# First layer's modulation with stationary conditions, and the attention's maximum and value products rewritten

## The chip, the core and the metric

The kernel runs on one core of one Trainium2 chip. Its time is the device time of one launch in microseconds (us), from the first instruction to the last. Each number of the trace comes from one profiled execution, taken by the hardware profiler. The engines are called PE (TensorE, matrix products), PEld (TensorE's loading of stationary weights), DVE (VectorE), ACT (ScalarE), POOL (GpSimd) and SP (SyncE, which issues the DMA transfers). SBUF is the on-chip memory of 128 partitions, PSUM the memory that TensorE writes.

## What is computed

One inference step of a trunk of two layers, for 1024 latent and 128 context tokens of width 1024. Each layer modulates its normalised input with shift, scale and gate, which are a linear map of the SiLU of a condition vector; there are two conditions, one for latent, one for context tokens. Layer 0 mixes tokens by attention, in which 8 heads of latent attention (96 wide) and 8 query heads of grouped attention (64 wide) stand side by side. Layer 1 mixes by a state-space scan and a gated linear unit. Each ends in a feed-forward block with a convolution. What the change touches is this part of the reference:

```python
def modulation(cond, w_mod, b_mod):
    m = jax.nn.silu(cond.astype(jnp.float32)) @ w_mod.astype(jnp.float32) + b_mod.astype(jnp.float32)
    return [t[:, None, :].astype(cond.dtype) for t in jnp.split(m, 6, axis=-1)]

def modulate(h, shift, scale):
    return h * (1 + scale) + shift
...
def attend(q, k, v):
    ...
    scale = 1.0 / math.sqrt(dq)
    def one_block(qi):
        s = jnp.einsum('bqgrd,bkgd->bgrqk', qi.astype(jnp.float32), kf) * scale
        p = jax.nn.softmax(s, axis=-1)
        return jnp.einsum('bgrqk,bkgd->bqgrd', p, vf)
```

## The kernel before

Tokens lie in nine tiles of 128 (eight latent, one context). Products of full precision are made of three products of rounded halves (`mm3`: high x high, high x low, low x high), so most operands exist as a high and a low tile (names ending in h and l). A product in plain float32 (`mm`) is two passes on TensorE, and the trace counts each pass as a matmul.

The stages run one after the other: the prologue (0 to 44 us), the input projection of layer 0 (44 to 313), attention (first transposes 334, last 940), the feed-forward block (960 to 1960), then layer 1.

**Modulation.** The map has six parts of 1024 columns, q = 0 to 5, and reads 1024 rows in eight blocks k of 128. Conditions and small vectors come into `vrows`, one row per 128 values, and are transposed into the columns of `vcol`. The first two parts (shift and scale of the first norm) are made in the prologue by `mod_part` (L125): the two condition columns of block k (`cond(k)`) are the stationary operand, 128x2, the weights move through, 512 columns at a time, all eight k into the same two rows of PSUM; two VectorE additions put the bias on (L135), eight products with a 2x2 unit matrix turn the result into columns, and one VectorE step writes A or B, by which the first norm's output is scaled and shifted. The next three parts (q = 2, 3, 4) are 24 pieces (`mod_piece`) in the projection's order. A piece fetches 128 columns of all 1024 rows (`ring`, 512 KB in runs of 512 bytes), uses them as eight 128x128 stationary operands, moves the two conditions through, and writes a 128x2 result by one VectorE step.

**Projection.** `Plan` (L2373 on) is a list scheduler: each step has an engine, a cost in us, a key (about when it is due), steps it depends on and buffers it takes. It writes one order for each engine, and the engines run it in that order. The keys are sums with the offsets of the table `TI`. The same planner orders attention, with the table `TM`.

**Attention.** There are 32 groups, one for each head and half of the latent queries; a group has four query tiles j and nine key tiles k (slots). For each j TensorE makes the scores in two parts, sa (768 keys) and sb (384 keys). VectorE takes the maximum of sa (L1041), then that of sb and the larger of both times the negative scale (L1046, L1047: `score_max_b`). ScalarE takes the exponentials into the buffer p (8 of them), sb's first (L1054), sa's then (L1061), both with that maximum as the bias. For each slot k TensorE transposes the four p tiles into one PSUM bank tb (L1070), ScalarE rounds it to pth (L1075), VectorE subtracts for the rest, ptl (L1081), and TensorE multiplies both with the values (`values`): v has 128 columns, the high and low halves of 64. In between stand the turning of the next heads' keys and queries (L931 to L946), the copies and outputs of a group (`pv_copy`, `finish_out`), and the context queries' small attention (`post1`, L1139 to L1142). GpSimd and VectorE also prepare constants of layer 1 (L1733 and others).

```python
            nc.vector.tensor_reduce(mx[:, 1:2], sb[:, :384], axis=AX.X, op=OP.max)
            nc.vector.scalar_tensor_tensor(mx[:, 2:3], mx[:, 0:1], mx[:, 1:2], nscale(hd), op0=OP.max, op1=OP.mult)
            ...
            self.mm(pv[:64], v[:, k, :64], l, False, False)
```

Of the kernel before, what the change touches and what calls it, by code (L numbers as in the profile page):

```python
# [8 lines left out]
F32 = mybir.dt.float32  # L9
# [7 lines left out]
D = 1024  # L17
NS = 8
NT = 9
KT = 8  # L20
# [6 lines left out]
TM = {"sa": -0.51, "sb": 1.2, "ma": -0.08, "mb": 0.77, "eb": 2.0, "ea": 3.1, "ta": 0.17, "td": 0.3, "v": 2.27, "pv": 0.25, "f0": 2.8, "f1": 0.1, "ss": 0.25, "pf": 0.0, "ph": 0.3, "pl": 0.6, "win": 0.2}  # L27
# [7 lines left out]
TI = {"win": 0, "hp": 0.34, "x": -3.37, "a": -1.34, "t": 0.99, "c": 2.74, "o": 3.21, "w": 4.11, "m": 3.93, "dm": 1.55, "st": 8.52, "ld": 8.94, "ml": -0.54}  # L35

class Trunk:
# [45 lines left out]
    def setup(self):  # L83
# [10 lines left out]
        rows = c.tile([72, 128], F32, name="vrows")  # L94
        nc.sync.dma_start(rows[0:8], I["c"].rearrange("o (k p) -> (o k) p", p=128))
        nc.sync.dma_start(rows[8:16], I["c_ctx"].rearrange("(k p) -> k p", p=128))
        nc.sync.dma_start(rows[16:32], I["norm1_g"].rearrange("l (k p) -> (l k) p", p=128))
        nc.sync.dma_start(rows[32:48], I["norm2_g"].rearrange("l (k p) -> (l k) p", p=128))
        nc.sync.dma_start(rows[48:72], I["b_mod"][0, 2 * D:5 * D].rearrange("(k p) -> k p", p=128))
        nc.scalar.activation(rows[0:16], rows[0:16], AF.Silu)  # L100
        self.vcol = c.tile([128, 72], F32, name="vcol")
# [7 lines left out]
        for l in range(2):  # L109
            for n in (1, 2)[l:]:  # L110
                self.A[l, n] = c.tile([128, 8, 2], F32, name=f"A{l}{n}")
                self.B[l, n] = c.tile([128, 8, 2], F32, name=f"B{l}{n}")
        self.vrows = rows

    def vec_cols(self, p):

        self.nc.tensor.transpose(p[:, :72], self.vrows, self.ident[:72, :72])
        self.nc.vector.tensor_copy(self.vcol, p[:, :72])
        b = self.vcol[:, 64:72]
        self.nc.vector.tensor_scalar(b, b, 1.0, None, op0=OP.add)  # L120

    def cond(self, k):
        return self.vcol[:, k:k + 9:8]

    def mod_part(self, w, bs, wk, ps2, psv, l, q):  # L125

        nc = self.nc
        rs = []
        for k in range(KT):
            for a in range(2):  # L130
                self.mm(ps2[a][0:2, :], self.cond(k), w(k)[:, a * 512:(a + 1) * 512], k == 0, k == KT - 1)
            yield
        for a in range(2):
            r = wk.tile([128, 512], F32, name="v_t")[0:2]
            nc.vector.tensor_tensor(r, ps2[a][0:2, :], bs[a], op=OP.add)  # L135
            if q in (2, 5):
                nc.sync.dma_start(self.m_rows[l, :, q, a * 512:(a + 1) * 512], r)
            rs.append(r)
        if q in (2, 5):
            return  # L140
        for j in range(KT):
            self.mm(psv[:, 2 * j:2 * j + 2], rs[j // 4][:, j % 4 * 128:(j % 4 + 1) * 128], self.ident[0:2, 0:2], True, True)
        n = 1 if q < 3 else 2
        src = psv[:, :16].rearrange("p (k c) -> p k c", c=2)
        if q % 3 == 0:
            nc.vector.tensor_copy(self.B[l, n], src)
        else:
            g0 = (16 if n == 1 else 32) + 8 * l
            g = self.vcol[:, g0:g0 + 8].unsqueeze(2).to_broadcast([128, 8, 2])
            nc.vector.scalar_tensor_tensor(self.A[l, n], src, 1.0, g, op0=OP.add, op1=OP.mult)  # L150
# [106 lines left out]
    def attn_in(self):  # L257
# [15 lines left out]
        ps = self.pool(st, "ai_ps", bufs=2, space=PSUM)  # L273

# [59 lines left out]

# [2542 lines left out]
```

## Time and profile before

| what | us |
|---|---|
| three runs: median (lowest, highest) | 3208.28 (3203.06, 3208.59) |
| profiled execution | 3213.05 |
| its span, first to last instruction | 3211.3 |
| PE busy in the span | 3078.6 (96%) |
| DVE busy | 2205.0 (69%) |
| ACT busy | 1509.7 (47%) |
| POOL busy | 1106.6 (34%) |

The shares are means over stages that differ, so the rows further below are taken from single stretches. A row of a timeline gives the start, the duration, the engine, the line of the kernel, the operation with output and inputs, its shape (for a matmul the stationary operand, then the moving one) and a count when several alike run together. Matmuls overlap, so a start is subtracted from the next start to get what one costs. A bracket names the idle time ahead of it and what ended that.

### The profile page before, as it was taken

Reading aid. Unit: us, or ns where it says so; the run is one execution under the profiler, and the core shown is the slowest. Engines: PE = TensorE matmul, PEld = TensorE weight load, DVE = VectorE, ACT = ScalarE, POOL = GpSimd, SP = SyncE. Lnnn points to the kernel's source line nnn. Section 1 sums busy time; section 2 is a strip of 40 time slices with the busy share of each in tenths; the row PEclk is TensorE's granted clock in tenths of the full one; section 3 lists DMA queues with packets and bytes.
Section 4 is the critical chain, followed back from the end, with each engine's and each line's share of the span. In section 5 each row is a group of like instructions: output and inputs, shape, how many; then the busy total and the mean of one; then the engine's idle time right before and its main releaser. Section 6 shows DMA issues by size and latency. Waiting matters only on the chain. (4 is left out here: it accounts for less than half of the span.)

```text
span 3211.3 us, 49583 instructions
## 1 busy us (share of the span) xinstructions
PE 3078.6 (96%) x18116; PEld 2771.4 (86%) x18116; DVE 2205.0 (69%) x3936; ACT 1509.7 (47%) x3027; POOL 1106.6 (34%) x1789
## 2 busy tenths in 40 slices
PE   8999888999999999999999998899999999999999
PEld 4999777788878898888888897779999999999998
DVE  3645888888864777887888967773365556656555
ACT  3421766677752344334444445662344444444443
POOL 2645566765022554164516404853320001001000
PEclk8999999999999999999999998999999999999999
DMA  5654212222121546544556646851133444444443
GB/s 207 191 166 122 46 59 74 67 72 96 48 71 60 165 147 199 158 148 147 178 156 197 197 137 165 210 149 55 53 99 120 130 122 141 121 128 139 124 131 99
DMA packets 535532, 408.75 MB, mean 127 GB/s; under 512 B 97765, under 2 KB 495733, under 8 KB 535289
## 3 DMA queue, kind: packets, MB, share of 16 engines
q1 hardware_dynamic: 535288, 405.58, 42.3%
q8 instruction: 143, 2.34, 0.3%
q14 instruction: 101, 0.82, 0.1%
HBM read 351.01 MB, written 54.51 MB: 126 GB/s over the span
## 5 line engine op out<-in xcount | busy, mean ns | idle before, releaser
L52 PE MATMUL ub<-hh,wu_l 128*128 128x386 f32 (+1 forms) x1056 | 359.2, 340 | 10.5 <-DVE wu_l L62 10.5
L52 PE MATMUL ua<-hh,wu_l 128*128 128x386 f32 (+1 forms) x1056 | 358.1, 339 | 0.4 <-DVE wu_l L62 0.4
L52 PE MATMUL ub<-hh,wu_h 128*128 128x386 f32 (+1 forms) x1056 | 357.6, 339 | 0.5 <-ACT wu_h L61 0.5
L52 PE MATMUL ua<-hl,wu_h 128*128 128x386 f32 (+1 forms) x1056 | 357.9, 339 | 0.0
L52 PE MATMUL ub<-hl,wu_h 128*128 128x386 f32 (+1 forms) x1056 | 357.8, 339 | 0.0
L52 PE MATMUL ua<-hh,wu_h 128*128 128x386 f32 (+1 forms) x1056 | 357.3, 338 | 0.2 <-DVE cv_a L2630 0.2
L62 DVE TENSOR_TENSOR wu_l<-wu_raw,wu_h 128x1024 fp32r<-128x1024 f32 x264 | 329.9, 1250 | 37.9 <-ACT wu_h L61 37.8
L2660 POOL TENSOR_TENSOR o<-o,f_h 128x512 f32<-128x512 f32 x16 | 21.7, 1373 | 864.7 <-DVE f_h L2673 864.7
L52 PE MATMUL y<-wd_h,g_h 128*128 128x512 f32 x792 | 319.2, 403 | 0.0
L52 PE MATMUL y<-wd_h,g_l 128*128 128x512 f32 x792 | 312.6, 395 | 0.0
L52 PE MATMUL y<-wd_l,g_h 128*128 128x512 f32 x792 | 312.1, 394 | 0.0
L61 ACT ACTIVATE wu_h<-wu_raw 128x1024 fp32r<-128x1024 f32 x264 | 276.5, 1047 | 32.4 <-PE sa L52 18.3
L2621 ACT ACTIVATE cv_a<-ua,cw 128x384 f32<-128x384 f32 (+1 forms) x132 | 88.7, 672 | 378.1 <-PE ua L52 378.1
L2621 ACT ACTIVATE cv_b<-ub,cw 128x384 f32<-128x384 f32 (+1 forms) x132 | 88.7, 672 | 337.1 <-PE ub L52 337.1
L1075 ACT ACTIVATE pth<-tb 128x512 fp32r<-128x512 f32 x288 | 171.5, 599 | 121.5 <-PE tb L1070 108.2
L1070 PE MATMUL tb<-ident,p 128*128 128x128 f32 x1152 | 178.6, 278 | 35.7 <-DVE ptl L1081 33.1
L52 PEld LDWEIGHTS ub<-hh,wu_l 128*128 128x128 f32 x1056 | 199.0, 188 | 15.2 <-DVE wu_l L62 15.2
L1081 DVE TENSOR_TENSOR ptl<-tb,pth 128x512 fp32r<-128x512 f32 x288 | 193.9, 683 | 26.0 <-ACT pth L1075 23.7
L2629 DVE SCALAR_TENSOR_TENSOR cv_a<-ua,cw,cv_a 128x384 f32<-128x384 f32 (+1 forms) x132 | 81.4, 617 | 182.4 <-ACT cv_a L2621 182.1
L52 PEld LDWEIGHTS ua<-hl,wu_h 128*128 128x128 f32 x1056 | 199.2, 189 | 5.9
L52 PEld LDWEIGHTS ua<-hh,wu_h 128*128 128x128 f32 x1056 | 199.0, 188 | 6.0 <-issue 0.5
L52 PEld LDWEIGHTS ub<-hh,wu_h 128*128 128x128 f32 x1056 | 199.2, 189 | 0.9 <-ACT wu_h L61 0.8
(561 smaller groups left out, 8280.9 us busy)
## 6 DMA issues: line engine op xcount, KB each, us to landing
wu_raw<-in_ffn_w_up_dram SPq DMA_DIRECT2D x264, 512.0 KB
wd_raw<-in_ffn_w_down_dram SPq DMA_DIRECT2D x132, 512.0 KB
mw<-in_w_mod_dram SPq DMA_DIRECT2D x28, 1024.0 KB
ring<-in_w_mod_dram SPq DMA_DIRECT2D x24, 512.0 KB
tab_s<-t_o SPq DMA_DIRECT2D x16, 584.0 KB
tb<-tab_s SPq DMA_DIRECT2D x64, 146.0 KB
m<-in_w_mod_dram SPq DMA_DIRECT2D x8, 1024.0 KB
ca_s<-o SPq DMA_DIRECT2D x16, 512.0 KB
```

What stands on the lines that cost most here:

```text
L52: return self.nc.tensor.matmul(out, lhsT, rhs, start=start, stop=stop)
L61: self.nc.scalar.activation(hi, src, AF.Copy)
L62: self.nc.vector.tensor_tensor(lo, src, hi.bitcast(F32), op=OP.subtract)
L1070: nc.tensor.transpose(t[:, j * 128:(j + 1) * 128], P[hd, a, j][:, k * 128:(k + 1) * 128], self.ident)
L1075: nc.scalar.activation(h, PT[hd, a, k][0], AF.Copy)
L1081: nc.vector.tensor_tensor(l, t, h.bitcast(F32), op=OP.subtract)
L2621: nc.scalar.activation(t[:, :m], p[:, 1:1 + m], AF.Identity, scale=cw[:, 1, cf:cf + 1], bias=cw[:, 3, cf:cf + 1])
L2629: nc.vector.scalar_tensor_tensor(t[:, :m], p[:, 0:m], cw[:, 0, cf:cf + 1], t[:, :m], op0=OP.mult, op1=OP.add)
L2660: e.tensor_tensor(x, x, s, op=OP.add)
```

## The change

**Prologue.** The conditions are copied into `cpad`, 32 columns for each k of which two are filled. `mod_part` holds `cpad[:, k]` stationary in the column tile of partitions 32(k mod 4), so that four k's write four stretches of PSUM partitions and two rounds cover eight. One half is copied out by VectorE, the other by ScalarE, and eight products with `sum4` (128x2, which has ones at the rows of the four tiles) turn and add at once. The bias is added afterwards, as columns, by `mod_set`. Its rows are now part of `vrows` (88 rows).

**Pieces.** A piece fetches 128 rows of all 1024 columns, in rows of 4 KB. It has four products: `cpad[:, n]` stationary in column tile j, 256 of the columns moving. VectorE adds the 128x256 result into `ACC`, and after the eighth piece of a part TensorE transposes `ACC` in two halves and `mod_set` writes the part.

**Attention.** The scale, with a minus sign, goes into the gains `g_gq` and `g_mq` with which the queries are normalised, so scores come out negated; the maximum becomes a minimum, and the exponential's scale is −1. `score_max_b` is one VectorE step that takes the elementwise minimum of sb with sa's minimum, writes it to p as scrap and accumulates the row's minimum. p is therefore taken in that step. The products of v with ptl use all 128 columns. The rotation of queries and keys works in place. The planner's costs and the offsets in `TM` and `TI` are other numbers.

```diff
-TM = {"sa": -0.51, "sb": 1.2, "ma": -0.08, "mb": 0.77, "eb": 2.0, "ea": 3.1, "ta": 0.17, "td": 0.3, "v": 2.27, "pv": 0.25, "f0": 2.8, "f1": 0.1, "ss": 0.25, "pf": 0.0, "ph": 0.3, "pl": 0.6, "win": 0.2}
+TM = {"sa": -1.14, "sb": -0.03, "ma": -1.2, "mb": 0.36, "eb": 1.57, "ea": 3.1, "ta": 0.34, "td": 0.3, "v": 2.27, "pv": 0.89, "f0": 2.8, "f1": 0.1, "ss": 0.35, "pf": 0.0, "ph": 0.3, "pl": 0.6, "win": 0.2}
...
+        nc.vector.tensor_copy(self.cpad[:, :, :2], self.vcol[:, :16].rearrange("p (c k) -> p k c", c=2))
...
+        nc.vector.tensor_reduce(self.sum4, self.ident.rearrange("p (j n) -> p n j", j=4)[:, :2], axis=AX.X, op=OP.add)
...
+        v.tensor_tensor(dst, src, cols(self.mod_bias(q)), op=OP.add)
+        if q in (1, 4):
+            g0 = 16 if q == 1 else 32
+            v.tensor_tensor(dst, dst, cols(self.vcol[:, g0:g0 + 8]), op=OP.mult)
...
-        for k in range(KT):
+        for k0 in (0, 4):
             for a in range(2):
-                self.mm(ps2[a][0:2, :], self.cond(k), w(k)[:, a * 512:(a + 1) * 512], k == 0, k == KT - 1)
-            yield
+                for k in range(k0, k0 + 4):
+                    o = 32 * (k - k0)
+                    self.mm(ps2[a][o:o + 32, :], self.cpad[:, k], w(k)[:, a * 512:(a + 1) * 512], k0 == 0, k0 > 0)
         for a in range(2):
-            r = wk.tile([128, 512], F32, name="v_t")[0:2]
-            nc.vector.tensor_tensor(r, ps2[a][0:2, :], bs[a], op=OP.add)
...
+            r = wk.tile([128, 512], F32, name="v_t")
+            if a:
+                nc.scalar.activation(r, ps2[a], AF.Copy)
+            else:
+                nc.vector.tensor_copy(r, ps2[a])
+            for j in range(4 * a, 4 * a + 4):
+                self.mm(psv[:, 2 * j:2 * j + 2], r[:, j % 4 * 128:(j % 4 + 1) * 128], self.sum4, True, True)
+        self.mod_set(q, (self.B if q == 0 else self.A)[0, 1], psv[:, :16].rearrange("p (k c) -> p k c", c=2))
...
+        g.tensor_scalar(g_gq, g_gq, -1.0 / math.sqrt(64), None, op0=OP.mult)
+        g.tensor_scalar(g_mq, g_mq, -1.0 / math.sqrt(96), None, op0=OP.mult)
...
-                w = S[name] = raw().rearrange("p (k n) -> p k n", k=KT)
-                nc.sync.dma_start(w, wm[:, :, q * D + n * 128:q * D + (n + 1) * 128])
+                w = S[name] = raw()
+                nc.sync.dma_start(w, wm[n, :, q * D:(q + 1) * D])
...
-                for k in range(KT):
-                    self.mm(p[:, :2], w[:, k], self.cond(k), k == 0, k == KT - 1)
+                for j in range(4):
+                    self.mm(p[32 * j:32 * j + 32, :256], self.cpad[:, n], w[:, 256 * j:256 * j + 256], True, True)
...
+                if n:
+                    v.tensor_tensor(ACC, p[:, :256], ACC, op=OP.add)
...
-            x = add("P", 1.75, key, mm, [l] + after, [pt], [rb])
+            x = add("P", .5, key, mm, [l] + after, [pt], [rb])
             mods.append(x)
-            x = add("D", .13, key, out, [x], [], [pt])
...
+            x = add("D", .36, key, out, [x] + ADDED[-1:], [] if n else [ACCB[q]], [pt, ACCB[q]] if n else [pt])
...
+                    for m in range(2):
+                        nc.tensor.transpose(p[:, m * 128:(m + 1) * 128], ACC[:, m * 128:(m + 1) * 128], self.ident)
...
-            nc.vector.tensor_reduce(mx[:, 1:2], sb[:, :384], axis=AX.X, op=OP.max)
-            nc.vector.scalar_tensor_tensor(mx[:, 2:3], mx[:, 0:1], mx[:, 1:2], nscale(hd), op0=OP.max, op1=OP.mult)
+            p = P[hd, a, j] = pk.tile([128, NK], F32, name="p", bufs=8)
+            nc.vector.tensor_scalar(p[:, 768:], sb[:, :384], mx[:, 0:1], None, op0=OP.min, op1=OP.min, accum_out=mx[:, 1:2])
...
-            self.mm(pv[:64], v[:, k, :64], l, False, False)
+            self.mm(pv, v[:, k, :], l, False, False)
...
-                mb = plan.add("D", .722, t + TM["mb"], lambda e=e, j=j: score_max_b(*e, j), [sb, ma], [], [B, mx])
-                eb = plan.add("A", .557 + .7 * more, t + TM["eb"], lambda e=e, j=j: score_exp_b(*e, j), [mb, ss[0] if j else None], [p] if j else [p, dn], [B, mx, dn] if j else [B, mx])
+                mb = plan.add("D", .57, t + TM["mb"], lambda e=e, j=j: score_max_b(*e, j), [sb, ma], [p], [B, mx])
+                eb = plan.add("A", .79 + .7 * more, t + TM["eb"], lambda e=e, j=j: score_exp_b(*e, j), [mb, ss[0] if j else None], [] if j else [dn], [B, mx, p, dn] if j else [B, mx, p])
```

The order of instructions moves at three places of interest. On VectorE, at the start of the program (pin and pt are PSUM banks, ring holds x tiles and weights, v_t the copied halves), before:

```order
3 L347 TENSOR_SCALAR ring<-ring,nrs 128x1024 x2
4 L135 TENSOR_TENSOR v_t<-pin,m_0_127 2x512 x2
5 L146 COPY B_81<-pt 128x16
6 L62 TENSOR_TENSOR wkvl<-ring,wkvh 128x864 x2
7 L62 TENSOR_TENSOR wkvl<-ring,wkvh 128x576
8 L347 TENSOR_SCALAR ring<-ring,nrs 128x1024
9 L135 TENSOR_TENSOR v_t<-pin,m_1_137 2x512 x2
10 L150 SCALAR_TENSOR_TENSOR A_80<-pt,vcol 128x16
11 L496 CAST hh<-h_f 128x256
```

and now:

```order
2 L126 COPY cpad<-vcol 128x8x2
3 L129 TENSOR_SCALAR vcol<-vcol 128x8 x2
4 L130 TENSOR_REDUCE sum_68<-ident 128x2
5 L368 TENSOR_SCALAR ring<-ring,nrs 128x1024 x2
6 L164 COPY v_t<-pin 128x512
7 L145 TENSOR_TENSOR B_75<-pt,vcol 128x16
8 L62 TENSOR_TENSOR wkvl<-ring,wkvh 128x864 x2
9 L62 TENSOR_TENSOR wkvl<-ring,wkvh 128x576
10 L368 TENSOR_SCALAR ring<-ring,nrs 128x1024
11 L164 COPY v_t<-pin 128x512
12 L145 TENSOR_TENSOR A_74<-pt,vcol 128x16
13 L148 TENSOR_TENSOR A_74<-A_74,vcol 128x16
```

The copy of q = 1 stands behind the third normalisation, as the two additions did. On TensorE, at the end of the projection (pin and pu take the projection's products, k_l and q_l are the first head's keys and queries), before:

```order
1212 L52 MATMUL pin<-wgbh,hl 128x384
1213 L52 MATMUL pt<-vcol,ring 128x2 x24
1214 L931 MATMUL tb<-ident,k_l 128x128 x10
1215 L931 MATMUL tb<-ident,q_l 128x128 x9
1216 L52 MATMUL sa<-kh,qh 128x384
```

and now:

```order
1214 L52 MATMUL pin<-wgbh,hl 128x384
1215 L52 MATMUL pt<-ring,cpad 32x256 x16
1216 L823 MATMUL pt<-ident,m_acc 128x128 x2
1217 L968 MATMUL tb<-ident,k_l 128x128 x10
1218 L968 MATMUL tb<-ident,q_l 128x128 x9
```

Three pieces of eight products stood behind the last projection, four of four products and the last turn stand there now. On VectorE, at the boundary of two early groups of attention (numbers tell buffers apart: sb_9927 is the next group's last score, tb_9905 and so on the slots of the running group), before:

```order
1177 L1041 TENSOR_REDUCE mx_9910<-sa_9895 128x1
1178 L1081 TENSOR_TENSOR ptl_9923<-tb_9905,pth_9914 128x512
1179 L1081 TENSOR_TENSOR ptl_9934<-tb_9916,pth_9925 128x512
1180 L1046 TENSOR_REDUCE mx_9910<-sb_9927 128x1
1181 L1047 SCALAR_TENSOR_TENSOR mx_9910<-mx_9910,nsc96_3534 128x1
1182 L1139 TENSOR_REDUCE mxp_9861<-sb_9927 128x1
1183 L1140 TENSOR_TENSOR mxp_9861<-mxp_9861,nsc96_3534 128x1
1184 L1142 RECIPROCAL rsp_9864<-mxp_9861 128x1
1185 L1081 TENSOR_TENSOR ptl_9961<-tb_9936,pth_9945 128x512
```

and now:

```order
1010 L1071 TENSOR_REDUCE mx_9190<-sa_9174 128x1
1011 L1150 TENSOR_TENSOR o_3404<-tb_9184,rs_8831 128x4x64
1012 L1109 TENSOR_TENSOR ptl_9209<-tb_9192,pth_9200 128x512
1013 L1109 TENSOR_TENSOR ptl_9220<-tb_9202,pth_9211 128x512
1014 L1109 TENSOR_TENSOR ptl_9238<-tb_9222,pth_9229 128x512
1015 L1077 TENSOR_SCALAR p_9249,mx_9190<-sb_9213,mx_9190 128x384
1016 L1109 TENSOR_TENSOR ptl_9251<-tb_9231,pth_9240 128x512
1017 L1167 TENSOR_REDUCE mxp_9157<-sb_9213 128x1
1018 L1169 RECIPROCAL rsp_9160<-mxp_9157 128x1
```

The step that takes a p buffer (p_9249) stands directly ahead of the subtraction of the ninth slot (tb_9231) of the group that last used that buffer; before, p was taken by ScalarE.

## Rows read from the trace of the kernel before

**Rows 1.** Stretch, its length; busy us of PE, PEld, DVE, ACT, POOL; clock, DMA share, GB/s.
```profile
100.00:150.00 50.00, 50.00 (x317) 46.76 (x316) 31.48 (x105) 20.30 (x53) 29.11 (x55) 0.99 0.69 214
345.00:928.00 583.00, 533.79 (x3410) 459.80 (x3408) 505.99 (x1004) 420.45 (x1037) 315.57 (x436) 0.99 0.23 67
```

**Rows 2.** TensorE's waits, 345 to 928: us in total, times, longest.
```profile
PE tb L1070 <- DVE ptl L1081: 30.9, 45, 2.4
...
PE tb L52 <- DVE ptl L1081: 4.1, 4, 2.4
```

**Rows 3.** Timeline of VectorE, end of the prologue: start us, us, operation, [idle before].
```profile
40.61 0.75 DVE L347 TENSOR_SCALAR ring<-ring,nrs 128x1024 f32<-128x1024 f32 x1 [3.45 <-POOL nrs L67]
41.28 1.27 DVE L135 TENSOR_TENSOR v_t<-pin,m 2x512 f32<-2x512 f32 x2
44.52 0.17 DVE L150 SCALAR_TENSOR_TENSOR A<-pt,vcol 128x16 f32<-128x16 f32 x1 [1.98 <-PE pt L52]
```

**Rows 4.** Timeline of TensorE, same place.
```profile
42.00 2.49 PE L52 MATMUL pt<-ident,v_t 2*128 2x2 f32 x16 [1.65 <-DVE v_t L135]
44.42 1.12 PE L487 MATMUL pt<-ident,ring 128*128 128x128 f32 x4
```

**Rows 5.** Timeline of TensorE, one modulation piece in the projection.
```profile
110.51 1.84 PE L52 MATMUL pt<-vcol,ring 128*128 128x2 f32 x16
112.21 0.31 PE L487 MATMUL pt<-ident,ring 128*128 128x128 f32 x1
```

**Rows 6.** Timeline of TensorE, end of the projection.
```profile
307.50 5.42 PE L52 MATMUL pt<-vcol,ring 128*128 128x2 f32 x48
313.34 1.94 PE L931 MATMUL tb<-ident,k_l 128*128 128x128 f32 x8 [0.42 <-issue]
319.04 0.69 PE L931 MATMUL tb<-ident,k_l 128*128 128x128 f32 x2 [3.76 <-DVE kh L946]
```

**Rows 7.** Timeline of TensorE in the state-space stage.
```profile
2071.28 1.22 PE L52 MATMUL v<-u,wit 128*64 128x146 f32 x16
2072.42 0.66 PE L1947 MATMUL st<-ident,wi 128*128 128x128 f32 x4
...
2073.36 0.67 PE L52 MATMUL y<-u,tt 128*128 128x146 f32 x4
2073.95 1.26 PE L52 MATMUL y<-xx,wo 64*128 64x146 f32 x16
```

**Rows 8.** VectorE's groups by line, 345 to 928: busy us, mean ns, idle before.
```profile
L1046 DVE TENSOR_REDUCE mx<-sb 128x1 f32<-128x384 f32 x120 | 66.0, 550 | 5.0 <-PE sb L52 4.0
...
L1047 DVE SCALAR_TENSOR_TENSOR mx<-mx,nsc 128x1 f32<-128x1 f32 x121 | 50.6, 418 | 4.3
```

**Rows 9.** Timeline of VectorE, one score step in attention.
```profile
338.13 0.56 DVE L1046 TENSOR_REDUCE mx<-sb 128x1 f32<-128x384 f32 x1
338.73 0.22 DVE L1047 SCALAR_TENSOR_TENSOR mx<-mx,nsc 128x1 f32<-128x1 f32 x1
338.86 1.28 DVE L1081 TENSOR_TENSOR ptl<-tb,pth 128x512 fp32r<-128x512 f32 x2
```

**Rows 10.** The page's costliest groups, whole span: one feed-forward step from PSUM.
```profile
L2629 DVE SCALAR_TENSOR_TENSOR cv_a<-ua,cw,cv_a 128x384 f32<-128x384 f32 (+1 forms) x132 | 81.4, 617 | 182.4 <-ACT cv_a L2621 182.1
```

**Rows 11.** Timeline of TensorE, first slot of a group and a later one.
```profile
337.03 0.48 PE L52 MATMUL pv<-pth,v_hl 128*128 128x512 f32 x1
337.35 0.39 PE L52 MATMUL pv<-ptl,v_hl 128*64 128x512 f32 x1
337.58 0.34 PE L52 MATMUL sb<-kh,qh 128*128 128x384 f32 x1
...
340.97 0.60 PE L1070 MATMUL tb<-ident,p 128*128 128x128 f32 x4
...
341.64 0.40 PE L52 MATMUL pv<-pth,v_hl 128*128 128x512 f32 x1
341.87 0.34 PE L52 MATMUL sa<-kh,qh 128*128 128x384 f32 x1
```

More of the change, by code (lines that the diff above doesn't have):

```diff
@@ L93, in setup @@
         nc.gpsimd.memset(self.mhalf, -0.5)
[L94 to L101, printed above, removed]
+        self.vcol = c.tile([128, 88], F32, name="vcol")
+        self.sum4 = c.tile([128, 2], F32, name="sum4")
         self.m_rows = self.dram.tile([2, 2, 6, D], F32, name="m_rows")
@@ L112, in setup, with vec_rows @@
                 self.B[l, n] = c.tile([128, 8, 2], F32, name=f"B{l}{n}")
+    def vec_rows(self, pool):
+        nc, I = self.nc, self.I
+        rows = pool.tile([88, 128], F32, name="vrows")
+        nc.sync.dma_start(rows[0:8], I["c"].rearrange("o (k p) -> (o k) p", p=128))
+        nc.sync.dma_start(rows[8:16], I["c_ctx"].rearrange("(k p) -> k p", p=128))
+        nc.sync.dma_start(rows[16:32], I["norm1_g"].rearrange("l (k p) -> (l k) p", p=128))
+        nc.sync.dma_start(rows[32:48], I["norm2_g"].rearrange("l (k p) -> (l k) p", p=128))
+        nc.sync.dma_start(rows[48:88], I["b_mod"][0, 0:5 * D].rearrange("(k p) -> k p", p=128))
+        nc.scalar.activation(rows[0:16], rows[0:16], AF.Silu)
@@ L332, in attn_in @@
         feed = Feed()
+        self.cpad = wp.tile([128, KT, 32], F32, name="cpad")
+        g.memset(self.cpad, 0.0)
         p = ps.tile([128, 512], F32, name="pt")
@@ L370, in attn_in @@
             pv = ps.tile([128, 512], F32, name="pt")
-            for i, _ in enumerate(self.mod_part(lambda k: MW[q][:, k], MB[q], wk, pm, pv, 0, q)):
-                pass
+            self.mod_part(lambda k: MW[q][:, k], wk, pm, pv, q)
             if q == 0:
@@ L579, in cross @@
                 s5 = src().rearrange("p n (a b c) -> p n a b c", a=2, b=2)
-                S[name, "u"] = u, _ = [wk.tile([128, 6 * 64], F32, name=f"rope_{i}", bufs=1)[:, :n * hd] for i in "uw"]
+                S[name, "u"] = u = wk.tile([128, 6 * 64], F32, name="rope_u", bufs=1)[:, :n * hd]
                 u5 = u.rearrange("p (n a b c) -> p n a b c", n=n, a=2, b=2)
@@ L761, in q_tile @@
             store(key + TI["o"] + 1, lambda: [(self.q_s[t], S.pop(("qt", t)).rearrange("p h c -> p (h c)"))], [y], [qk])
-        gate_c = wp.tile([128, 2, KT], F32, name="gate_c")
-        wm = I["w_mod"][0].rearrange("(k p) n -> p k n", p=128)
+        gate_c = wp.tile([128, KT, 2], F32, name="gate_c")
+        wm = I["w_mod"][0].rearrange("(k p) n -> k p n", p=128)
         gates, mods = [], []
+        ACC = wp.tile([128, 256], F32, name="m_acc")
+        ACCB = {}
         def mod_piece(q, n, key, after):
@@ L1128, in prompt @@
             ps = passes(hd)
-            mx = wk.tile([128, 3], F32, name="mxp", bufs=2)
+            mx = wk.tile([128, 2], F32, name="mxp", bufs=2)
             p = wk.tile([128, 128], F32, name="pp")
```

139 lines of the change are left out of this document (64 added, 75 removed).

## The prediction

> **What bounds the kernel now.** I read the busy time of the engines by stretches first, then the waits of the engine that comes out full, then single stretches of its timeline, since the change touches three places and an average over the run hides each of them. In the projection (100 to 150 us as a sample) TensorE is busy 50.00 of 50 us, VectorE 31.5 [rows 1]. A microsecond of TensorE work removed there is a microsecond gained, and work added on VectorE or the DMA queues (share 0.69) has room. In attention (345 to 928) TensorE is busy 533.8 of 583 us and VectorE 506.0: neither full, both close [rows 1]. The waits say how they are tied. TensorE waits 30.9 + 4.1 = 35 us, 49 times, for ptl, the low half of the transposed probabilities, which VectorE writes (L1081) [rows 2]. So 35 of its 49 idle us are VectorE being late, and VectorE is late because it is 87% busy with steps in a fixed order. The prologue is a third thing: a chain of single steps, read step by step [rows 3, 4]. What runs behind attention, some 2250 us, is not edited, and I leave its time alone.
>
> **The change, part by part.**
>
> *The prologue's modulation (q = 0, 1).* Its end is what counts. In before x's third tile is normalised on VectorE at 40.61, the two additions for q = 1 run 41.28 to 42.55 (1.27 us for two), the small products take TensorE from 42.00 to 44.42, A is written at 44.52 in 0.17 us [rows 3, 4]. The order of the changed kernel still has that normalisation (L368) ahead of q = 1's copy (L164) on VectorE, so nothing behind it starts sooner, however fast the column-tiled products have become; their end is hidden behind the wait for x. After it: one copy on VectorE (half of 1.27, 0.64) and the other on ScalarE at the same time; 8 sum products, again 16 passes, now with a 128x128 stationary block instead of 2x128. Their price lies between the present 2.42 us (44.42 − 42.00) and 3.4: passes with a 128x128 load take 1.70/16 = 0.106 us at a granted clock of 0.99 [rows 5, 1], and at half of that clock 16 of them take 3.4. Then two VectorE steps instead of one, 0.2 more. Saved 0.6, added 0.2 to 1.2 and a handover to ScalarE: **+1 us**, with −1 and +3 as bounds. cpad's fill, sum4 and the bias additions stand before the first weights arrive, the scalings of the gains are two short GpSimd steps before their first use: nil. Without that cover they are under ten steps of 0.2 us, inside the bounds.
>
> *The 24 pieces (q = 2, 3, 4).* One piece now: 16 passes of 2 columns, each with its own 128x128 weights, 110.51 to 112.21 = 1.70 us [rows 5]. Before the last input projection ends (307.50) there are 21; three run together behind it, 5.42 us for 48 passes [rows 6]. These hide: the keys' transposes come at 313.34, and the next ones wait until 319.04 for kh, at the end of a chain of store and reload that starts with the last projection [rows 6]. So 21 x 1.70 = 35.7 us are on the path.
>
> A new piece is 4 products, 8 passes, of 256 columns on four column tiles. No row shows four. Two are shown in the state-space stage: 16 passes of 146 columns on two tiles take 2071.28 to 2072.42 = 1.14 us, while 4 full-width passes of the same length take 2073.36 to 2073.95 = 0.59, so that 16 would be 2.36 [rows 7]. Two tiles do run at once, by a factor of 2.1. For four I must choose. Each product is two passes on one tile, one behind the other, and TensorE takes its instructions in order: the second pass of a tile waits for its first, and the next tile's first can only join that second. That gives two in flight, whatever the number of tiles. Scaled: 1.14 x 8/16 x 256/146 = 1.0, plus 0.1 for entering and leaving the tiled form: **1.1 us**. The bounds are half of 1.0, 0.5 (four at once), and 2.36 x 8/16 x 256/146 = 2.1 (one at a time). In the changed order 20 pieces and two turns (two transposes each, about 0.25 us) stand before the end of the last projection: 20 x 1.1 + 0.5 = 22.5, so **−13 us**. Four at once: 10.5, −25. One at a time: 42.5, +7.
>
> VectorE's addition into ACC costs no more than a step of 512 columns, 0.64 us [rows 3], 24 times in a stage where that engine has 18.5 of 50 us free [rows 1]. Each of the first two turns makes TensorE wait for the last addition if little is queued between; half a microsecond each is inside the bounds. The third turn, and the four pieces behind the last projection, hide as the three did. The fetch is 512 KB as before, in rows of 4 KB; TensorE does not starve for weights in the sample, so a quicker fetch gives nothing.
>
> *Attention, the maximum.* Before, its second half is a reduction of 128x384 (120 in this stretch, mean 550 ns) and a step on one column (mean 418 ns) [rows 8]. In a quiet place the small one takes 338.73 to 338.86 = 0.13 us until the next start, the pair 0.73 [rows 9]; the mean pair is 0.97. Now it is one step on 128x384 that reads PSUM, writes the p buffer and accumulates the minimum. No row has it; the reduction (550 ns) and the 128x384 step with a column operand from PSUM (617 ns [rows 10]) are its neighbours: **0.58 us**. For 128 pairs that saves 128 x 0.15 = 19 us against the quiet pair and 128 x 0.39 = 50 against the mean one; should the new step cost as much as the quiet pair, 0 to 31. What the path gets back is at most the waits that VectorE causes, 35 of TensorE's 49 idle us.
>
> How much of the 35? The relief comes once per score step, 4 in each group of 9 slots: 0.6 to 1.6 us per group, while the wait on ptl is 35/32 = 1.1 us per group, up to 2.4 at once [rows 2]. They are of one size, and the waits pile up where VectorE is several steps behind. Two thirds, **−23 us**, is my choice; the rest stays as handover. Bounds 0 and −45 (nearly all idle time of TensorE).
>
> *Attention, full-width value products.* v's product with ptl fills 128 columns instead of 64. Behind transposes, four of them and both value products go from 340.97 to 341.87, 0.90 us; two full-width products at 0.23 and four transposes at 0.11 give the same, so there is nothing to gain. In the first slot of a group the product with pth (128 columns) comes first: 337.03 to 337.35 is 0.32, then 0.23 to 337.58 [rows 11]. This switch costs 0.09 us, 32 times: **−3 us**. The Trainium skill, TensorEngine Tiling (Array Packing), Key Properties, says that changing the tiling mode drains the engine. By it all 288 narrow products would lose something, 26 us at 0.09 each; the 0.90 us show no such loss at most of them.
>
> Attention in all −26, between −3 and −48. Rotating in place and the new planner costs change order, not work.
>
> **The sum.** −13 + 1 − 26 = −38. The profiled execution took 3213.05 us, so 3175 for one like it; it is 4.8 above the median of 3208.28, and the same steps give **3170 us** for the median.
>
> **The rivals.**
>
> A. *Four tiles at once.* A piece takes 0.5 us, the projection gives −25: 3158. For it: two tiles gain their full factor [rows 7]. Against: the two passes of a product follow each other on one tile. The Trainium skill, TensorEngine Tiling (Array Packing), Theoretical Speedup, gives up to 4 times for 32 columns; no row here shows it.
> B. *The relief is not on the path.* VectorE sheds its time, but ScalarE's pth or the scores become what is late: attention gives −3 to −12, in all −15 to −24, 3190. For it: VectorE itself idles 77 of the 583 us [rows 1], so it is late by order, not by load.
> C. *Tiles do not overlap here.* A piece takes 2.1 us, the projection +7, in all −18: 3190. Against: [rows 7].
> D. *Slower.* The p buffer is now taken on VectorE at the maximum, not on ScalarE at the exponential. There are 8, two groups' worth. In the changed order the first maximum of a group stands right before the last ptl of the group two ahead of it, and that slot's transposes on TensorE are the last to read the buffer it takes. VectorE, in order, holds this ptl and all behind it until TensorE has transposed, and TensorE then waits for the ptl. There are 31 such boundaries, and the price is up to the longest wait seen now, 2.4 us [rows 2]: 74 us, 3170 + 74 = 3244. It decides from 38/31 = 1.2 us per boundary. Against: the transposes are issued a slot before VectorE's subtraction needs them, so the buffer should be free about when VectorE comes to it.
>
> **How the numbers follow.** The forecast 0.54, A 0.15, B 0.14, C 0.07, D 0.10. The first four are faster; what a measurement of this kernel can tell from no change is about 0.2%, 6.4 us, and B and C with the other bounds against them come inside it at times, as does a mild D. Faster 0.85, same 0.06, slower 0.09. The range goes from A with attention 20 us better (3138, rounded to 3139) to B or C with another 10 us lost (3200); D and the far ends are left out.
>
> **What would show it.** In the profile of the changed kernel: pieces 1.1 us long and the last input projection some 13 us sooner; the new step near 0.58 us and VectorE's busy time in attention down by 19 to 50; TensorE's waits on ptl down from 35 to about 12; even distances in the first slots; A within 3 us of 44.5. Pieces of 0.5 speak for A, of 2.1 for C. If VectorE's load falls and TensorE's idle time stays under another name, it is B. If VectorE waits on TensorE's transposes ahead of the new step at group ends, it is D; over 1.2 us each, and the forecast is wrong.

## The result, and the profile after

The changed kernel takes 3167.0 us (median of 4 runs, 3160.65 to 3171.72) against 3208.44 for the kernel before: a ratio of 0.987 with a 95% interval of 0.9847 to 0.9894, 41 us less. Forecast were 3170 and a range of 3139 to 3200. The profiled execution of the changed kernel took 3160.65 us, its fastest, that of before 3213.05, slower than any timed run of it, so the two traces lie 52 us apart.

TensorE's timeline cuts both traces at the same five places (us): the first product of the input projection, the first transposes of attention, the first product of the feed-forward block (1054.9 in before; the output projection lies ahead of it), the first of the state-space stage, and the first of layer 1's feed-forward block. The last row ends with VectorE's last step.

| stretch | before | after | difference |
|---|---|---|---|
| start to the first projection product | 49.0 | 49.6 | +0.6 |
| from there to attention's first transposes | 285.4 | 262.9 | −22.5 |
| attention and output projection | 720.4 | 695.5 | −24.9 |
| feed-forward block | 908.0 | 908.5 | +0.5 |
| state-space stage | 395.7 | 389.5 | −6.2 |
| the rest, to VectorE's last step | 848.6 | 849.0 | +0.4 |

The state-space stage is not edited. In the traces of the runs below, each with this stage unchanged, it took 387 to 396 us in no relation to the edit; the 6.2 us are scatter between executions. What the change did lies in two stretches.

Busy us in the two sampled stretches of the changed kernel (the stretch and its length, then PE, PEld, DVE, ACT, POOL with their counts, the granted clock, DMA share, GB/s); they answer to [rows 1], and 323 to 888 is about the same part of attention as 345 to 928 there (120 score steps in each):

```profile
100.00:150.00 50.00, 50.00 (x315) 43.05 (x314) 37.68 (x122) 21.77 (x55) 33.99 (x63) 1.00 0.75 243
323.00:888.00 565.00, 529.77 (x3444) 466.31 (x3442) 478.73 (x996) 424.50 (x1049) 320.03 (x441) 1.00 0.26 71
```

In the projection TensorE is full as before, and VectorE carries 6 us more in 50. In attention VectorE went from 506.0 to 478.7 us, TensorE from 49 to 35 us of idle time in a stretch that is 18 us shorter. TensorE's waits there (total us, times, longest), which answer to [rows 2]:

```profile
PE tb L1098 <- DVE ptl L1109: 14.6, 24, 1.8
PE tb L968 <- DVE kl L981: 4.4, 8, 1.1
PE tb L1098 <- DVE ql L981: 3.0, 10, 0.5
...
PE tb L968 <- DVE ptl L1109: 1.9, 3, 1.0
...
PE tb L52 <- DVE ptl L1109: 1.1, 1, 1.1
```

The waits on ptl fell from 36 us to 17.6. Some of the room was taken by other VectorE work: the low halves of the next head's keys (kl) and queries (ql) now end waits of 8.4 us (with a row of 1.0 that is not shown), against 2.9 in before.

One piece of the modulation on TensorE, answering to [rows 5], and the end of the projection, answering to [rows 6]:

```profile
105.23 0.40 PE L52 MATMUL pu<-wukvh,trl 128*128 128x512 f32 x1
105.55 0.64 PE L52 MATMUL pt<-ring,cpad 128*32 128x256 f32 x8
106.12 0.50 PE L52 MATMUL pu<-wukvh,trh 128*128 128x512 f32 x1
106.46 0.39 PE L52 MATMUL pu<-wukvl,trh 128*128 128x512 f32 x1
```

```profile
285.36 1.07 PE L52 MATMUL pt<-ring,cpad 128*32 128x256 f32 x16
289.91 0.67 PE L52 MATMUL pt<-ring,cpad 128*32 128x256 f32 x8 [3.47 <-DMA ring<-in_w_mod_dram]
291.18 1.08 PE L52 MATMUL pt<-ring,cpad 128*32 128x256 f32 x8 [0.60 <-DMA ring<-in_w_mod_dram]
292.79 0.69 PE L823 MATMUL pt<-ident,m_acc 128*128 128x128 f32 x2 [0.54 <-DVE m_acc L809]
293.84 1.94 PE L968 MATMUL tb<-ident,k_l 128*128 128x128 f32 x8 [0.36 <-DVE A L145]
```

A piece now takes 105.55 to 106.12 = 0.57 us, and all of the 20 pieces that stand between projections take 0.57. The distances beside it grow too: the product ahead takes 0.32 us to the next start and the one behind 0.34, where products of this kind follow each other by 0.23 elsewhere. So a piece costs 0.77 us on the path, 15.2 us for the 20. A piece of before had nothing extra ahead of it and, in most cases, 0.09 behind: 1.79 us. Behind the last projection two of the four left wait for weights (3.47 and 0.60 us) and the turn waits for VectorE; the keys' transposes start at 293.84, 8.5 us after the last projection's end at 285.36, against 5.8 before, and the distance from there to attention's first transposes is 27 us in both kernels. So these waits are hidden, as forecast.

The end of the prologue on VectorE and on TensorE, answering to [rows 3, 4]:

```profile
40.21 0.75 DVE L368 TENSOR_SCALAR ring<-ring,nrs 128x1024 f32<-128x1024 f32 x1 [3.39 <-POOL nrs L67]
40.88 0.68 DVE L164 COPY v_t<-pin 128x512 f32<-128x512 f32 x1
45.23 0.17 DVE L145 TENSOR_TENSOR A<-pt,vcol 128x16 f32<-128x16 f32 x1 [3.67 <-PE pt L52]
45.44 0.18 DVE L148 TENSOR_TENSOR A<-A,vcol 128x16 f32<-128x16 f32 x1
```

```profile
41.62 3.57 PE L52 MATMUL pt<-sum,v_t 128*128 128x2 f32 x16 [9.35 <-DVE v_t L164]
45.05 1.10 PE L506 MATMUL pt<-ident,ring 128*128 128x128 f32 x4
```

The sum products take 41.62 to 45.05 = 3.43 us instead of 2.42, A is done at 45.62 instead of 44.69. The granted clock over these products is 0.50, in before it was 0.75 over 42.00 to 44.42. One score step on VectorE, answering to [rows 9], and its groups by line, answering to [rows 8]:

```profile
339.42 0.61 DVE L1077 TENSOR_SCALAR_CACHE_REDUCE p<-sb,mx 128x384 f32<-128x384 f32 x1
339.95 0.08 DVE L1077 DVE_READ_ACCUMULATOR p<-sb,mx 128x1 f32 x1
339.95 0.69 DVE L1109 TENSOR_TENSOR ptl<-tb,pth 128x512 fp32r<-128x512 f32 x1
```

```profile
L1077 DVE TENSOR_SCALAR_CACHE_REDUCE p<-sb,mx 128x384 f32<-128x384 f32 x120 | 72.9, 608 | 4.9 <-PE sb L52 3.1 <-PE tb L1098 1.3
...
L1077 DVE DVE_READ_ACCUMULATOR p<-sb,mx 128x1 f32 x120 | 9.9, 82 | 0.0
```

The new step has two records, the pass and the reading of its accumulator. From its start to the next operation's start it takes 339.42 to 339.95 = 0.53 us, against 0.73 for the pair before; the median of the 86 in this stretch that the next operation follows without idle time is 0.53 as well. Its record of 0.61 us overlaps the next one.

### The profile page after: what moved, and what is told of

Read it like the earlier page. It is cut to its first block, busy times and chain, and to the rows that moved or that the text cites. A ratio compares the mean times of both kernels' runs of the same rounds, so it can differ in the third digit from the quotient of the medians.

```text
span 3158.8 us, 49364 instructions
## 1 busy us (share of the span) xinstructions
PE 3026.1 (96%) x17930; PEld 2728.6 (86%) x17930; DVE 2174.9 (69%) x3924; ACT 1510.8 (48%) x3029; POOL 1103.6 (35%) x1792
## 5 line engine op out<-in xcount | busy, mean ns | idle before, releaser
L2687 POOL TENSOR_TENSOR o<-o,f_h 128x512 f32<-128x512 f32 x16 | 21.7, 1373 | 862.2 <-DVE f_h L2700 862.2
L52 PEld LDWEIGHTS ua<-hh,wu_l 128*128 128x128 f32 x1056 | 198.9, 188 | 1.0 <-DVE wu_l L62 1.0
```

The costliest lines, as they stand in the source:

```text
L52: return self.nc.tensor.matmul(out, lhsT, rhs, start=start, stop=stop)
L2687: e.tensor_tensor(x, x, s, op=OP.add)
```

## The experiments

The measure in all is the stretch from attention's first transposes to the first feed-forward product ("attention" below, 720 us before, 695.5 after), beside the total. The ratios are to runs of the kernel before on the same chip.

| kernel | total, us | ratio to before | projection | attention | PE idle in it |
|---|---|---|---|---|---|
| before (its trace) | 3208.44 | 1 | 285.4 | 720.4 | 53.2 |
| after | 3167.0 | 0.987 [0.9847, 0.9894] | 262.9 | 695.5 | 37.6 |
| mod_only (stretches of mod_only_again) | 3189.03 | 0.9929 [0.9912, 0.9945] | 267.0 | 715.9 | 52.0 |
| attn_only | 3185.45 | 0.9919 [0.9904, 0.9934] | 282.2 | 694.9 | 37.2 |
| max_two | 3184.36 | 0.9914 [0.9898, 0.9929] | 266.6 | 713.5 | 53.8 |
| old_table | 3201.2 | 0.9971 [0.9957, 0.9985] | 267.6 | 732.9 | 61.2 |
| narrow | 3167.48 | 0.9855 [0.9838, 0.9871] | 265.4 | 698.2 | 39.7 |
| old_plan_inplace | 3166.35 | 0.9857 [0.9834, 0.988] | 264.9 | 696.7 | 36.4 |
| old_plan (one run) | 3167.34 | | 266.0 | 699.6 | 40.0 |
| old_table_inplace (one run) | 3194.27 | | 266.6 | 723.4 | 58.4 |
| new_inplace (one run) | 3172.64 | | 266.5 | 697.4 | 40.4 |
| tiles_grouped (one run) | 3164.27 | | 265.0 | 697.1 | 39.0 |
| tiles_mixed (one run) | 3161.52 | | 264.9 | 696.9 | 38.8 |

With the changed modulation the projection takes 262.9 to 267.6 us, with the old one 282.2 and 285.4. The trace of the changed kernel is the lowest of its kind; about 18 us is the difference of the means. Attention is 720.4 and 715.9 us with the old attention and 694.9 to 697.1 in the four traces with the new one unaltered: about 22 us between the means.

**Each part alone.** mod_only is the changed kernel with attention's edits, costs and offsets put back:

```diff
-TM = {"sa": -1.14, "sb": -0.03, "ma": -1.2, "mb": 0.36, ...}
+TM = {"sa": -0.51, "sb": 1.2, "ma": -0.08, "mb": 0.77, ...}
...
-            nc.vector.tensor_scalar(p[:, 768:], sb[:, :384], mx[:, 0:1], None, op0=OP.min, op1=OP.min, accum_out=mx[:, 1:2])
+            nc.vector.tensor_reduce(mx[:, 1:2], sb[:, :384], axis=AX.X, op=OP.max)
+            nc.vector.scalar_tensor_tensor(mx[:, 2:3], mx[:, 0:1], mx[:, 1:2], nscale(hd), op0=OP.max, op1=OP.mult)
...
-            self.mm(pv, v[:, k, :], l, False, False)
+            self.mm(pv[:64], v[:, k, :64], l, False, False)
```

attn_only is the reverse, these edits made in the kernel before. The offsets `TI` and the rotation in place stay with the modulation's part and were not taken apart from it. Expected of mod_only:

> The modulation and projection part alone (prologue, pieces, their planner costs and table), attention as before. If the two parts are separate, the first transposes of attention come at about 312.5 us as in the changed kernel (before 334.5) and the stretch from there to the first feed-forward product stays at the 720 us of before: 3208 - 22 = 3186 us. If part of the gain in attention came from what the projection leaves behind (clock, transfers), that stretch gets shorter here too, below 715.

of its second run, for the trace, since the execution of mod_only that was profiled took 9694 us, three times the others, and is not used:

> The modulation part alone once more, for its trace: first transposes at 312 to 315 us, the stretch from there to the first feed-forward product 720 us as in before, with old offsets and costs in attention. Below 715 the projection's change would act into attention.

and of attn_only:

> The attention part alone (scale in the gains, one-step minimum, full-width value products, costs and table), modulation as before. Separate parts: first transposes at 334, the stretch to the first feed-forward product 695 us instead of 720, in all 3208 - 25 = 3183. If attention's gain depends on the changed projection, it stays above 3190.

Measured: 3189 and 3185 us, each within 3 us or so of what separate parts would give; mod_only_again took 3184.01 against 3210.16 for the kernel before. Its first transposes come at 316.9 us, 2 us later than its range, and its attention is 4 us shorter than in before. Attention's row in mod_only_again's trace, then in attn_only's:

```profile
316.90:1032.80 715.90, 663.93 (x4086) 566.21 (x4084) 564.33 (x1081) 462.06 (x1120) 354.23 (x492) 1.00 0.22 65
```

```profile
330.30:1025.20 694.90, 657.73 (x4087) 572.20 (x4085) 531.24 (x1065) 460.66 (x1120) 354.38 (x492) 1.00 0.24 67
```

The parts are separate within the scatter: attention stays at 716 with the old attention and at 695 with the new one, whatever the modulation. The two gains add to 22.8 + 26.4 = 49 us by these medians, some us more than the 41 by which the whole change was measured (44 in narrow below, which differs by a width without effect); the intervals are some 10 us wide or more, so this is no contradiction.

**VectorE's relief or the order.** max_two keeps the changed kernel but makes the minimum in two steps; p is then first written by ScalarE, which new_inplace below shows to change nothing in this order:

```diff
-            nc.vector.tensor_scalar(p[:, 768:], sb[:, :384], mx[:, 0:1], None, op0=OP.min, op1=OP.min, accum_out=mx[:, 1:2])
+            nc.vector.tensor_reduce(mx[:, 1:2], sb[:, :384], axis=AX.X, op=OP.min)
+            nc.vector.tensor_tensor(mx[:, 1:2], mx[:, 0:1], mx[:, 1:2], op=OP.min)
```

> The changed kernel, but the second half of the minimum in two VectorE steps again (a reduction of 128x384 and a minimum on one column), all engines' orders else as in the changed kernel; p is then taken by ScalarE again. Theory that VectorE's relief is what attention gained: VectorE's busy time rises by 20 to 40 us, TensorE's waits on ptl go from 18 back towards 35, the stretch of 695 us grows by 12 to 20, total about 3182. Rival that the new order brought the gain: the stretch stays within 4 us of 695, total within 5 us of 3167.

Attention's row and TensorE's waits in this kernel:

```profile
315.70:1029.20 713.50, 659.66 (x4086) 570.37 (x4084) 557.71 (x1065) 464.70 (x1120) 353.95 (x492) 1.00 0.24 65
```

```profile
PE tb L1099 <- DVE ptl L1110: 27.0, 32, 2.3
PE tb L968 <- DVE kl L981: 7.2, 8, 1.4
...
PE tb L968 <- DVE ptl L1110: 3.0, 6, 1.1
...
PE tb L52 <- DVE ptl L1110: 1.3, 2, 0.8
```

VectorE is busy 25 us longer (557.7 against 532.6 in the stretch of the table), the waits on ptl are back at 31 us, attention is 18 us longer. So about 18 of the 25 us of attention come from the step itself, in the new order (TensorE's idle time, 37.6 us in the changed kernel, is back at 53.8, and before it was 53.2).

old_table is the changed kernel with the old offsets in attention's table:

```diff
-TM = {"sa": -1.14, "sb": -0.03, "ma": -1.2, "mb": 0.36, ...}
+TM = {"sa": -0.51, "sb": 1.2, "ma": -0.08, "mb": 0.77, ...}
```

> The changed kernel with the old numbers in attention's table of offsets, all operations and costs new. Theory of the relief: most of the gain stays, the stretch from the first transposes to the first feed-forward product is under 705 us, total under 3177. Rival that the order brought it: the stretch is 713 to 722 us, total 3185 to 3195.

It came out above both: attention 733 us, 13 more than before the change, with the shorter step in it. Its row, and VectorE's waits on the scores:

```profile
316.70:1049.70 733.00, 671.82 (x4087) 568.08 (x4085) 530.64 (x1065) 463.27 (x1120) 354.62 (x492) 0.99 0.23 63
```

```profile
DVE mx L1071 <- PE sa L52: 19.3, 20, 2.7
DVE p L1077 <- PE sb L52: 16.3, 32, 0.7
```

These two waits sum to 35.6 us, 16.0 in the changed kernel: the scores come late there. By this run alone one would say that the order brought everything. The next four put that right.

**The old order with the short step.** In three of these four, the step's scrap is written over the scores in PSUM, so that p can be taken by ScalarE at the exponential as before; the exponentials of sb then read clipped scores, with the same amount of work:

```diff
-            p = P[hd, a, j] = pk.tile([128, NK], F32, name="p", bufs=8)
-            nc.vector.tensor_scalar(p[:, 768:], sb[:, :384], mx[:, 0:1], None, op0=OP.min, op1=OP.min, accum_out=mx[:, 1:2])
+            nc.vector.tensor_scalar(sb[:, :384], sb[:, :384], mx[:, 0:1], None, op0=OP.min, op1=OP.min, accum_out=mx[:, 1:2])
...
+            P[hd, a, j] = pk.tile([128, NK], F32, name="p", bufs=8)
```

old_plan_inplace has this with the old offsets and the old costs, old_plan the old offsets and costs with p taken by VectorE as changed. Expected of the first:

> The changed kernel with the old offsets and old costs in attention's plan, and p taken by ScalarE at the exponential as before: the one-step minimum writes its scrap over the scores in PSUM instead (the exponentials of sb are then of clipped scores, so this part of the result is left wrong). It is the order of before with only VectorE's step shortened. Theory of the relief: the stretch from the first transposes to the first feed-forward product, 720 us in before, falls to 697 to 708. Rival that the relief alone is not on the path: 714 to 720.

and of the second:

> The changed kernel with the old offsets and old costs in attention's plan, p taken by VectorE as changed. The price of taking p early in the old order is the difference to the run with p taken by ScalarE. Theory that the early p costs the old order its gain (rival D of the prediction): 15 us or more in the stretch of attention. Rival that old offsets with new costs were only a bad mix: within 6 us of the run with p taken by ScalarE.

Attention's rows of the two:

```profile
314.50:1011.20 696.70, 660.27 (x4085) 571.03 (x4084) 532.95 (x1065) 460.63 (x1120) 354.43 (x492) 1.00 0.24 66
```

```profile
315.40:1015.00 699.60, 659.63 (x4086) 571.38 (x4085) 532.31 (x1065) 462.16 (x1120) 354.32 (x492) 1.00 0.24 66
```

The theory of the relief holds: with the old plan the short step brings attention from 716 (mod_only_again) to 697, and the total to that of the changed kernel. It is not quite alone: the scale in the gains also saves the context queries a scaling step (in before 15 of 0.2 us, 3 us of VectorE in 345 to 928), and the value products are wide, which narrow below shows to be worth nothing. Taking p early costs 3 us there, not 15, and 3 us is no more than the scatter. The new offsets and costs are worth 4 us at most (699.6 against 695.5), about the scatter.

old_table_inplace and new_inplace do the same with the old offsets and new costs, and with the new offsets and new costs:

> The changed kernel with the old offsets, new costs, and p taken by ScalarE at the exponential, the scrap written over the scores in PSUM (the exponentials of sb are of clipped scores, that part of the result is left wrong). With the old offsets and p taken by VectorE the stretch was 733 us. Theory that taking p early is what the old offsets could not bear: below 712. Rival that offsets and costs don't fit each other, whoever takes p: above 725.

> The changed kernel with the new offsets and costs, but p taken by ScalarE at the exponential, the scrap written over the scores in PSUM (the exponentials of sb are of clipped scores, that part of the result is left wrong). If the early p costs nothing under the new offsets, as the one wait of 1.3 us on TensorE's transposes says, the stretch stays at 692 to 699 us. If it still costs, it falls below 690.

```profile
316.30:1039.70 723.40, 665.02 (x4085) 567.22 (x4084) 529.42 (x1065) 462.65 (x1120) 353.23 (x492) 1.00 0.23 64
```

```profile
316.20:1013.60 697.40, 656.99 (x4086) 570.00 (x4085) 534.04 (x1065) 460.58 (x1119) 352.55 (x492) 1.00 0.24 66
```

With the new offsets the early p costs nothing (697.4 against 695.5). With old offsets and new costs it costs 10 us (733 against 723) in one trace each, of which the granted clock makes up a part (by stretches of 10 us, 5.1 us of clock are lost in old_table, none in old_table_inplace). The 723 show that this mix is bad whoever takes p; neither expectation was met. Why the new costs make so poor an order of the old offsets was not followed further, and stays open.

**The width of the value products.** narrow is the changed kernel with

```diff
-            self.mm(pv, v[:, k, :], l, False, False)
+            self.mm(pv[:64], v[:, k, :64], l, False, False)
```

> The changed kernel with the product of v and ptl on 64 columns again. By the distances in the rows (0.09 us in the first slot of a group, nothing behind transposes) TensorE's busy time in attention rises by 3 us and the total by 0 to 3, inside the scatter. If every narrow product cost a drain, 288 of them would add some 26 us: 3193.

```profile
315.10:1013.30 698.20, 658.48 (x4086) 570.61 (x4085) 532.04 (x1065) 460.25 (x1120) 353.44 (x492) 1.00 0.24 66
```

The total is that of the changed kernel, and TensorE's busy time in the stretch is 658.5 us against 657.9. The first slot of a group there, and in the changed kernel, answering to [rows 11]:

```profile
319.25 0.48 PE L52 MATMUL pv<-pth,v_hl 128*128 128x512 f32 x1
319.57 0.40 PE L52 MATMUL pv<-ptl,v_hl 128*64 128x512 f32 x1
319.81 0.34 PE L52 MATMUL sb<-kh,qh 128*128 128x384 f32 x1
```

```profile
316.74 0.48 PE L52 MATMUL pv<-pth,v_hl 128*128 128x512 f32 x1
317.05 0.39 PE L52 MATMUL pv<-ptl,v_hl 128*128 128x512 f32 x1
317.28 0.34 PE L52 MATMUL sb<-kh,qh 128*128 128x384 f32 x1
```

The distance behind the product with pth is 0.32 us when the next product is narrow and 0.31 when it is full. It stands at either width behind transposes, so it is not a price of the width.

**The column tiles.** tiles_grouped has eight products of 128 columns in a piece, the two of a tile one behind the other; tiles_mixed the same products tile by tile in turn:

```diff
-                for j in range(4):
-                    self.mm(p[32 * j:32 * j + 32, :256], self.cpad[:, n], w[:, 256 * j:256 * j + 256], True, True)
+                for j in range(4):
+                    for c in (0, 128):
+                        self.mm(p[32 * j:32 * j + 32, c:c + 128], self.cpad[:, n], w[:, 256 * j + c:256 * j + c + 128], True, True)
```

> The changed kernel with each piece in eight products of 128 columns, both products of a column tile one behind the other (tile order 0 0 1 1 2 2 3 3). If TensorE lets a later tile's pass start past one that waits for its own tile, a piece stays at 0.55 to 0.7 us. If it goes strictly in program order, the four passes of a tile run alone but for one overlap with the next, 13 turns of 0.107 us, 1.4 us and more, and the projection ends some 17 us later.

> As the run with grouped tiles, but in the tile order 0 1 2 3 0 1 2 3. Both theories let the four tiles overlap as in the changed kernel: 0.55 to 0.7 us a piece. It is the yardstick for the grouped order: what the smaller products alone cost.

One piece of each, grouped first:

```profile
105.96 0.66 PE L52 MATMUL pt<-ring,cpad 128*32 128x128 f32 x16
106.56 0.50 PE L52 MATMUL pu<-wukvh,trh 128*128 128x512 f32 x1
```

```profile
106.31 0.65 PE L52 MATMUL pt<-ring,cpad 128*32 128x128 f32 x16
106.88 0.50 PE L52 MATMUL pu<-wukvh,trh 128*128 128x512 f32 x1
```

0.59 to 0.60 and 0.57 to 0.58 us in all 20 pieces of each. The order of the products in the program doesn't matter; four tiles work at once in either.

## Why the prediction was right, and where it was not

The total was right, with a term too small and another that does not exist. By the means of the traces the projection gives −18 and attention −22, 40 in all, against −13 and −26 in the forecast: one was too small by 5, the other too large by 4. That they cancel, and that the total lies nearer to the forecast's 3170 than to rival A's 3158, is luck.

**The pieces: the term was mis-sized.** Forecast 1.1 us each, measured 0.57. The step that failed is "That gives two in flight, whatever the number of tiles". It rested on the two passes of a product having to follow each other with the next tile joining the second. In the trace the passes of one piece start in two sets of four: at 105.553, 105.560, 105.567 and 105.573, then from 105.793 on. With 0.57 the prediction's own sum gives 20 x 0.57 + 0.5 − 35.7 = −23.8; with the prices on the path, 0.77 and 1.79, it is 20 x 0.77 + 0.5 − 21 x 1.79 = −21.7. The 0.1 us that the prediction added for entering and leaving the tiled form stood on no row: the distances show 0.09 ahead of a piece and 0.11 behind, and 0.09 of the latter was there before. −22.5 stands in the pair of traces, about −18 between the means of all runs, in which new waits of a few us take some of it back (4.0 us for the first tiles' h_f at the projection's start in the changed kernel, 2.6 before). This is rival A, to which 0.15 was given, and what the Trainium skill's up to 4 times for 32 columns (TensorEngine Tiling (Array Packing), Theoretical Speedup) says; the trace agrees. 8 passes in 0.57 us against an estimate of 2.07 one at a time (2.36 x 8/16 x 256/146 [rows 7]) is a factor of 3.6.

**The prologue: right.** +1 forecast, +0.6 measured at the first projection, which is no more than the scatter (48.1 us in attn_only, with the old prologue; 49.1 to 49.9 in the traces with the new one). The 3.43 us of the sum products is the upper of the two prices.

**The maximum: right in kind, and near in size.** 0.58 forecast, 0.53 measured. VectorE was to shed 19 to 50 us; in the stretch of the table it shed 31.8, 25 of them by the step itself (max_two). −23 was chosen as two thirds of the waits; the runs show 18 in the new order (max_two) and 16 to 19 in the old one. The waits on ptl fell to 17.6 us, not 12; kl and ql took their place in part.

**The wider value products: wrong.** −3 forecast, nothing measured (narrow). The step that failed read 0.32 us behind pth [rows 11] as a switch of width. The same row is there at full width.

**The clock: not in the sum.** Both attention stretches hold 4086 matmul records, yet TensorE is busy 667.2 us in before and 657.9 after. Four stretches of 10 us in before (the first two hold one place), with the whole stretch last, and below the one such stretch after, again with the whole:

```profile
420.00:430.00 10.00, 7.07 (x42) 5.60 (x40) 9.34 (x19) 6.51 (x18) 9.61 (x9) 0.95 0.00 0
430.00:440.00 10.00, 8.46 (x47) 7.30 (x47) 8.44 (x17) 5.71 (x14) 9.53 (x10) 0.88 0.01 2
470.00:480.00 10.00, 9.70 (x59) 8.79 (x58) 6.31 (x16) 6.78 (x24) 0.00 (x0) 0.84 0.00 0
600.00:610.00 10.00, 8.39 (x45) 7.12 (x45) 8.20 (x17) 6.73 (x22) 8.83 (x13) 0.83 0.00 1
334.50:1054.90 720.40, 667.20 (x4086) 569.34 (x4085) 564.47 (x1081) 461.80 (x1120) 354.31 (x492) 0.99 0.22 64
```

```profile
400.00:410.00 10.00, 7.14 (x40) 6.48 (x39) 9.18 (x20) 4.89 (x13) 9.53 (x10) 0.83 0.00 1
312.50:1008.00 695.50, 657.92 (x4086) 572.33 (x4084) 532.64 (x1065) 460.85 (x1120) 354.35 (x492) 1.00 0.24 67
```

The granted clock (the third column from the end) falls where TensorE had been idle, and what runs then takes longer. In before TensorE waited 2.40 us until 428.64, 2.38 until 469.37, and 0.86 and 1.37 until 599.88 and 604.92; behind the last, four transposes at 606.89 take 1.12 us, and 0.66 at full clock. Three such places became one: summed over these stretches, 10 x (0.05 + 0.12 + 0.16 + 0.17) = 5.0 us of lost clock against 1.7. This gain of 3 us is not the change's: mod_only_again, with the attention of before, loses 1.7 us too, max_two with its long step nothing, narrow with the short one 3.4. It differs from execution to execution, so before's trace overstates attention's gain by some 3 us. Of the 9.3 us of busy time 6 stand against mod_only_again as well (663.9); what they are was not followed and stays open.

**The rivals.** B, the relief not on the path, is ruled out by max_two and old_plan_inplace. C, no overlap, by the pieces' 0.57 us. D, the early p, has its row in the changed kernel among VectorE's waits (total, times, longest):

```profile
DVE p L1077 <- PE tb L1098: 1.3, 1, 1.3
```

One wait of 1.3 us, not 31 of 1.2 or more. Under the new offsets the early p has no price. The 10 us of old_table against old_table_inplace are a price of the early p, but not shown to be D's mechanism: ahead of the new step VectorE's waits there name the scores (16.3 us) and never the transposes. Against D stood in the prediction that the transposes run ahead; under the new offsets this is what happened.

## What to carry to other kernels

Where an engine that is 87% busy sets when another one waits, a shorter step on it gives back a part of those waits, here 16 to 19 of the 36 us under the name of ptl, for the 25 to 32 us that the engine shed, and the order need not be made anew for that. Offsets and costs of a scheduler belong together: new costs with the old offsets made attention slower (723 and 733 us) than the old set (700) or the new (695); the other mix was not run. And before a distance between two instructions is put down to their shape, look for the same distance where the shape is equal.

## What the runs showed of the hardware that was not expected

Four column tiles of 32 columns run at once in full: in the two pieces at 285.36, passes of 256 columns start in sets of four, 0.216 us apart, where one full-width pass of 146 columns takes 0.148 alone [rows 7], an estimated 0.26 for 256. The order of the products in the program, grouped by tile or in turn, made 0.59 or 0.57 us. Going from full-width products into a piece costs 0.09 us more than going on at full width (0.32 against 0.23); whether that is the change of tiles or the new weights is not shown. A product that fills 64 of 128 columns between full ones costs the same as a full one, 288 times over: the Trainium skill's sentence that a change of tiling mode drains the engine (TensorEngine Tiling (Array Packing), Key Properties) has no measurable price in these products. A small product with a 128x128 stationary block took 0.214 us a pass at the clock of the prologue's end (3.43 us for 16, clock 0.50 over 41.62 to 45.05), 0.106 at full clock [rows 5].
